# The first adaLN weights and the inputs, loaded in blocks of 256 columns

## The chip, the cores and the metric

The kernel runs on one core of one Trainium2 chip. The metric is the time of one execution on the device in microseconds (us). A core has the engines PE (TensorE: matrix products and transposes), ACT (ScalarE), DVE (VectorE), POOL (GpSimd) and SP (SyncE, which here only issues DMAs). They run side by side and wait for one another by semaphores. Sixteen DMA engines move data between the device memory and the on-chip memory, which has 128 partitions. PE writes to a separate accumulation memory of eight banks.

## The reference

One layer of a diffusion trunk on 128 context tokens and 512 latent tokens of width 1024, all in float32:

```
mod = silu(c) @ w_ada + b_ada             # 1024 x 6144; once for c, once for c_ctx
sh1, sc1, g1, sh2, sc2, g2 = split(mod)   # six pieces of 1024
h = x * (1 + sc1) + sh1
z = h @ w_in                              # 1024 x 3328, for three groups of heads
m = concat(attention A, gated recurrence B, attention C)(z) @ w_out
x = LN(alpha * x + g1 * m)
hid = relu((x * (1 + sc2) + sh2) @ w_ff1) ** 2
y = LN(alpha * x + g2 * (hid @ w_ff2))
```

Before anything of `w_in` can be multiplied, a block of 128 columns of the inputs needs its pieces of `sc1` and `sh1`, and these need their columns of `w_ada` over all 1024 rows.

## The kernel before, in words

The 640 tokens and the 1024 columns are cut into tiles of 128: `NT` = 5 tiles of tokens (tile 0 is the context) and `NK` = 8 blocks of columns. To reach float32 accuracy, each operand of a large product is split into a high and a low part (`split`: ACT copies the high part, DVE subtracts), and each product is three matmuls (`mm3`).

The change lies in the first stage, some 57 us long, a loop over the eight blocks j:

- `ada_load(j)` loads the columns of `sc1` and `sh1` of block j: two tiles of four row tiles each, two DMAs for each tile (256 KB, rows of 512 B), so 1 MB in four DMAs, all issued by SP. `x_load(j)` loads 128 columns of the inputs in two DMAs (64 and 256 KB). Three blocks are loaded ahead of the loop, and round j issues block j + 3. There are buffers for six blocks of weights and four of x.
- PE, block by block: `ada_rows` multiplies the conditioning with the 256 columns (sixteen instructions in the profile, `psada_s`); four transposes of the latent tiles of x (`psx`) and one of the context tile (`psm`); four small matmuls (L270, L271) that turn the adaLN rows into columns `sc1`, `sh1`.
- ACT scales and shifts the transposed block (`xm`, L275 and L276) and rounds it to `xh`; DVE subtracts for `xl`.
- `first_gemm(j - 2)` follows two blocks behind (`LAG` = 2): the products of block j - 2 with three columns of tiles of `w_in` (forget gates and q of group B, `wfq`), summed over all blocks in five banks `acc`. Their weights are loaded in rounds 0, 1, 3 and 5.

Behind the loop, PE multiplies the values of group B (`psib`, weights `wib`), and DVE and ACT work on the gates that come out of `acc`; `wfb` and `wq` are the next weights and `wad` the later columns of `w_ada`, in DMAs of 512 KB with 256 columns in a row (`ada_part`). All weights of `w_in` pass through `wslots`: two raw buffers, then the split into five buffers. SP issues in its own order, so a DMA that waits for a buffer holds those behind it. Six small constants (`scanm`, `rope_c`, `rope_s`, `gng`, `qng`, `kng`) are loaded by SP behind the stage.

What sets the order: in the loop the order on PE is written out by hand (`manual_schedule`). The other engines' order in the loop, and all engines' order behind it up to the output projection at some 420 us, is found by a planner when the kernel is built; it takes the program's order and estimated times, and lets an instruction that is ready pass one that waits. From the second half of the output projection on, all but POOL are in hand-written order again.

Of the kernel before, what the change touches and what calls it, by code (L numbers as in the profile page):

```python
# [11 lines left out]
F32 = mybir.dt.float32  # L12
# [7 lines left out]
P = 128  # L20
D = 1024
NK = D // P
NTOK = 640
NT = NTOK // P
# [38 lines left out]
def hybrid_layer_kernel(ctx: ExitStack, tc: tile.TileContext, T):  # L63
# [26 lines left out]
    def split(hi, lo, src):  # L90
        A.copy(hi, src)  # L91
        V.tensor_tensor(lo, src, f32(hi), op=ALU.subtract)  # L92
# [78 lines left out]
    with ExitStack() as sctx:  # L171
        sp = sctx.enter_context(tc.tile_pool(name="startsb", bufs=1, reuse_waits="tile"))

        crow = sp.tile([32, P], F32, tag="crow", name="crow")
        rows = sp.tile([37, P], F32, tag="rows", name="rows")
        nc.sync.dma_start(crow[0:8, :], T["c"])
        nc.scalar.dma_start(crow[8:16, :], T["c_ctx"])
        G.memset(cs.rearrange("p a b -> p (a b)"), 0.0)
        nc.scalar.dma_start(ident, T["k_ident"])
        nc.scalar.dma_start(crow[16:32, :], T["b_ada8"][0:16, :])  # L180
        ps0 = pp.tile([P, 512], F32, tag="misc", name="ps_rows", bufs=NMISC)
        PE.transpose(ps0[:, 0:32], crow, ident[0:32, 0:32])
        b1c = sp.tile([P, 16], F32, tag="b1c", name="b1c")
        V.tensor_copy(b1c, ps0[:, 16:32])
        sil = sp.tile([P, 16], F32, tag="sil", name="sil")
        sg = sp.tile([P, 16], F32, tag="sg", name="sg")
        A.activation(sg, ps0[:, 0:16], AF.Exp, scale=-1.0)
        V.tensor_scalar_add(sg, sg, 1.0)
        V.reciprocal(sg, sg)
        V.tensor_tensor(sil, ps0[:, 0:16], sg, op=ALU.mult)  # L190
        silv = sil.rearrange("p (v k) -> p k v", v=2)
        V.tensor_copy(cs[:, :, 0:2], silv)
        V.tensor_copy(cs[:, :, 16:18], silv)
        V.tensor_tensor(selc, ident[:, 0:2], ident[:, 32:34], op=ALU.add)
        V.tensor_tensor(selc, selc, ident[:, 64:66], op=ALU.add)
        V.tensor_tensor(selc, selc, ident[:, 96:98], op=ALU.add)

        def ada_load(j):
            parts = []
            for s in range(2):  # L200
                raw = sp.tile([P, 4, 2, P], F32, tag="adar0", name=f"adaw{j}_{s}", bufs=12)
                for i, c0 in enumerate((D + j * P, j * P)):
                    nc.sync.dma_start(
                        raw[:, :, i, :],
                        T["w_ada"][s * 512 : (s + 1) * 512, c0 : c0 + P].rearrange("(k p) n -> p k n", p=P),
                    )
                parts += [raw[:, k].rearrange("p a b -> p (a b)") for k in range(4)]
            return parts

        def x_load(j):  # L210
            x_j = sp.tile([P, NT, P], F32, tag="x", name=f"x{j}", bufs=4)
            csl = slice(j * P, (j + 1) * P)
            nc.sync.dma_start(x_j[:, 0, :], T["x_prompt"][:, csl])
            nc.sync.dma_start(x_j[:, 1:NT, :], T["x_sample"][:, csl].rearrange("(t p) n -> p t n", p=P))
            return x_j

        ahead = 3
        LAG = 2
        ada_q, x_q = [], []
        for j in range(ahead):  # L220
            ada_q.append(ada_load(j))
            x_q.append(x_load(j))
        acc = [pp.tile([P, 512], F32, tag=f"acc{i}", name=f"acc{i}") for i in range(5)]
        w01 = []

        def first_load(s):
            w01.extend(wslots(f"wfq{s}", T["w_in"], ((COL_FF, P), (COL_FB, P), (COL_QB, P)), 2, row0=s * 2 * P, nslot=1, swap=True))

        def first_gemm(j, cols):
            for i in cols:  # L230
                h, l = (w[:, i * P : (i + 1) * P] for w in w01[j])
                for st, mv, first, last in ((h, xh, True, False), (h, xl, False, False), (l, xh, False, True)):
                    PE.matmul(acc[i][:, 0:384], st, mv[:, j, 0:384], start=first and j == 0, stop=last and j == NK - 1)
                    PE.matmul(acc[3 + i // 2][:, i % 2 * 256 : i % 2 * 256 + 256], st, mv[:, j, 384:NTOK],
                              start=first and j == 0 and i != 1, stop=last and j == NK - 1 and i > 0,
                              skip_group_check=True)

        with tc.manual_schedule(engines={mybir.EngineType.PE}):
            for j in range(NK):
                ada, x_j = ada_q[j], x_q[j]  # L240
                if j in WPOS:
                    first_load(WPOS.index(j))
                if j + ahead < NK:
                    ada_q.append(ada_load(j + ahead))
                    x_q.append(x_load(j + ahead))
                if j == 2:
                    nc.gpsimd.dma_start(rows[0:8, :], T["ln1_g8"])
                    nc.gpsimd.dma_start(rows[8:16, :], T["ln1_b8"])
                    nc.gpsimd.dma_start(rows[16:17, :], T["subln_g"])
                    nc.gpsimd.dma_start(rows[17:21, 0:HD], T["lb_logits_fwd"])  # L250
                    nc.gpsimd.dma_start(rows[17:21, HD:P], T["lb_logits_bwd"])
                    nc.gpsimd.dma_start(rows[21:37, :], T["b_ada8"][24:40, :])
                    mf = sp.tile([P, 4 * CH], F32, tag="mf", name="mf")
                    nc.gpsimd.dma_start(mf, T["k_masks"])
                    G.tensor_copy(masks.rearrange("p a b -> p (a b)"), mf)
                if j == 6:
                    ps1 = pp.tile([P, 512], F32, tag="misc", name="ps_rows1", bufs=NMISC)
                    PE.transpose(ps1[:, 0:37], rows, ident[0:37, 0:37])
                    V.tensor_copy(colc, ps1[:, 0:37])
                    V.tensor_scalar_add(colc[:, 29:37], colc[:, 29:37], 1.0)  # L260
                r = sp.tile([P, 2 * P], F32, tag="adar", name=f"adar{j}", bufs=2)
                ada_rows(r, pp.tile([P, 512], F32, tag="ada", name=f"psada_s{j}", bufs=NADA), ada)
                px = pp.tile([P, 512], F32, tag="xt", name=f"psx{j}", bufs=NXT)
                for t in range(1, NT):
                    PE.transpose(px[:, (t - 1) * P : t * P], x_j[:, t, :], ident)
                pm = pp.tile([P, 512], F32, tag="misc", name=f"psm{j}", bufs=NMISC)
                PE.transpose(pm[:, 0:P], x_j[:, 0, :], ident)
                if j >= LAG:
                    first_gemm(j - LAG, (0,))
                PE.matmul(pm[:, P : P + 2], r[:, 0:P], selc, start=True, stop=True)  # L270
                PE.matmul(pm[:, P + 2 : P + 4], r[:, P : 2 * P], selc, start=True, stop=True)  # L271
                V.tensor_scalar(sc1[:, j, :], pm[:, P : P + 2], b1c[:, 8 + j : 9 + j], 1.0, op0=ALU.add, op1=ALU.add)
                V.tensor_scalar(sh1[:, j, :], pm[:, P + 2 : P + 4], b1c[:, j : j + 1], None, op0=ALU.add)
                xm = sp.tile([P, NTOK], F32, tag="xm", name=f"xm{j}", bufs=2)
                A.activation(xm[:, 0:P], pm[:, 0:P], AF.Identity, scale=sc1[:, j, 1:2], bias=sh1[:, j, 1:2])  # L275
                A.activation(xm[:, P:NTOK], px, AF.Identity, scale=sc1[:, j, 0:1], bias=sh1[:, j, 0:1])  # L276
                split(xh[:, j, :], xl[:, j, :], xm)
                if j >= LAG:
                    first_gemm(j - LAG, (1, 2))
            for j in range(NK - LAG, NK):  # L280
                first_gemm(j, range(3))
# [712 lines left out]
    gr, parts, tok, wks = {}, {}, {}, {}  # L994
# [102 lines left out]
    for h in range(NHA):  # L1097
        for t in range(1, NT):
            n = h * nu + t - 1
# [42 lines left out]
    for t in range(1, NT):  # L1142
        for j in range(4):
            n = NHA * nu + (t - 1) * 4 + j
# [60 lines left out]
    raws = {(i, j): rawp.tile([P, 4, HALF], F32, tag=f"q{i}{j}", name=f"q{i}{j}") for j in range(2) for i in range(2)}  # L1205
# [433 lines left out]
    for u in range(2, NU):  # L1639
# [32 lines left out]
        else:  # L1672
            c12(u - 1)

            f = f12[0].rearrange("p a k n -> p a (k n)")
# [71 lines left out]
    for n in range(2):  # L1747
# [6 lines left out]
        for m, i in enumerate(order):  # L1754
            if n == 0 and m < 4:
                continue
            if i % 2 == 0:
                w = next(ws)
                raw = ep.tile([P, 2, 512], F32, tag=f"wr{w % NWR}", name=f"wg{n}_{i}r")
# [111 lines left out]
```

## Time and profile before

| | |
|---|---|
| median of 3 runs | 940.05 us (936.37 to 941.13) |
| profiled execution | 940.01 us |
| its span, first to last instruction | 938.2 us |
| busy: PE, DVE, ACT, POOL | 880.3, 665.1, 474.9, 69.0 us |
| mean granted clock of PE | 0.975 of full speed |
| moved from and to device memory | 96.24 and 12.58 MB |

All times in the rows are microseconds from the start of the span unless marked ns. A busy PE is not PE at its peak, since matmuls overlap. The granted clock is 1.00 (2.4 GHz) or 0.50 (1.2 GHz); a mean between the two comes from a change inside the stretch. The DMA share is the mean busy share of the core's 16 DMA engines; it goes above 1 where packets overlap.

### The profile page before, as it was taken

To read this page: it belongs to the slowest core of one execution; us is meant where nothing else is said; L and a number is where in the kernel's file an instruction comes from. 1 tells how busy PE (TensorE), PEld (TensorE's weight loads), DVE (VectorE), ACT (ScalarE), POOL (GpSimd) and SP (SyncE) were. 2 spreads that over 40 slices of the span, in tenths; PEclk is the share of its full clock that TensorE was granted. 3 is DMA by queue.
4 is the path that set the end of the run, shared out by engine and by line. 5 is a ranking of instruction groups with operands and counts; after the bars stand their busy time and mean duration, and the time that the engine had idled before them with its cause. 6 is when DMAs were issued, how large, how long until landed. Compare 5 with 4: busy or idle time off the path is not lost.

```text
span 938.2 us, 15408 instructions
## 1 busy us (share of the span) xinstructions
PE 880.3 (94%) x5941; PEld 762.6 (81%) x5941; DVE 665.1 (71%) x1232; ACT 474.9 (51%) x973; POOL 69.0 (7%) x136
## 2 busy tenths in 40 slices
PE   5989898999999998999988899999998999999996
PEld 3878786789889786677778899988997888888885
DVE  2369997988876878886579877676762874574448
ACT  3567665466664638761566544453553633243320
POOL 2200010210101010001000100110000000000000
PEclk7999998999999999999999999999999999999998
DMA  9951525432122211007102543456325863052202
GB/s 261 287 168 50 179 71 146 118 95 69 55 58 62 68 51 57 2 28 274 36 1 64 186 145 134 157 176 208 129 79 188 295 218 99 22 177 90 67 22 92
DMA packets 102314, 109.84 MB, mean 117 GB/s; under 512 B 6720, under 2 KB 82208, under 8 KB 102240
## 3 DMA queue, kind: packets, MB, share of 16 engines
q1 hardware_dynamic: 96256, 92.33, 32.0%
q0 software_dynamic: 5792, 16.44, 5.0%
q8 instruction: 47, 0.77, 0.3%
q14 instruction: 27, 0.22, 0.1%
q10 hardware_dynamic: 192, 0.08, 0.0%
HBM read 96.24 MB, written 12.58 MB: 116 GB/s over the span
## 4 chain that ended last, share of the span: by engine, by line
PE 67%; DVE 15%; DMA 8%; ACT 6%; issue 3%; SPq 1%; DVEq 0%; ACTq 0%
PE psx L1453 10%; PE psy L131 8%; PE psy L129 8%; PE psy L130 8%; PE psz L1453 5%; DMA wad<-in_w_ada 3%; PE psA L130 2%; PE psA L129 2%; PE psA L131 2%; PE psavA L731 2%; DVE b_st L561 2%; PE psy L1453 2%; DMA wf_r<-in_w_ff 2%; PE psavC L953 1%; DVE b_lqk L516 1%
## 5 line engine op out<-in xcount | busy, mean ns | idle before, releaser
L92 DVE TENSOR_TENSOR gl<-hidb,gh 128x640 fp32r<-128x640 f32 x54 | 43.7, 821 | 49.1 <-ACT gh L91 49.0
L91 ACT CAST gh<-hidb 128x640 fp32r<-128x640 f32 x54 | 38.6, 728 | 69.3 <-PE psy L130 61.9
L1453 PE MATMUL psx<-s,wf3h 128*128 128x320 f32 x256 | 58.9, 317 | 6.2 <-ACT kept L1459 3.0
L129 PE MATMUL psA<-wa_h,xh 128*128 128x384 f32 x160 | 54.9, 344 | 0.0
L131 PE MATMUL psA<-wa_h,xl 128*128 128x384 f32 x160 | 54.5, 342 | 0.0
L130 PE MATMUL psA<-wa_l,xh 128*128 128x384 f32 x160 | 54.2, 340 | 0.0
L1459 ACT COPY kept<-psx 128x320 f32<-128x320 f32 x48 | 20.5, 427 | 65.6 <-PE psx L1453 65.6
L1453 PEld LDWEIGHTS psx<-s,wf3h 128*128 128x128 f32 x256 | 44.1, 193 | 7.0 <-ACT kept L1459 3.3
L1340 DVE TENSOR_TENSOR wf3l<-wf_t,wf3h 128x2048 fp32r<-128x2048 f32 (+2 forms) x20 | 37.2, 1864 | 9.0 <-ACT wf3h L1336 9.0
L1453 PE MATMUL psx<-s,wf3l 128*128 128x320 f32 x128 | 40.3, 315 | 0.0
L1472 DVE TENSOR_TENSOR st<-psz,kept 128x320 f32<-128x320 f32 x32 | 15.7, 489 | 26.2 <-ACT kept L1459 13.7
L129 PE MATMUL pswo<-wo,mxh 128*128 128x512 f32 x80 | 32.1, 403 | 0.4 <-ACT wo L91 0.4
L130 PE MATMUL pswo<-wo,mxh 128*128 128x512 f32 x80 | 31.7, 397 | 0.8 <-DVE wo L92 0.8
L709 DVE TENSOR_REDUCE nmA<-pssA 128x1 f32<-128x768 f32 x32 | 30.2, 951 | 2.2 <-PE pssA L707 1.8
L129 PEld LDWEIGHTS psA<-wa_h,xh 128*128 128x128 f32 x160 | 30.1, 188 | 1.9 <-issue 1.2
L1336 ACT CAST wf3h<-wf_t 128x2048 fp32r<-128x2048 f32 (+2 forms) x20 | 30.9, 1554 | 1.3 <-DVE wf_t L1312 0.9
L131 PE MATMUL pswo<-wo,mxl 128*128 128x512 f32 x80 | 31.5, 393 | 0.0
L1518 POOL DMA_DIRECT2D hd<-st x28 | 15.3, 546 | 219.3 <-ACT st L1465 120.4
L711 ACT ACTIVATE pA<-pssA,nmA 128x768 f32<-128x768 f32 x32 | 28.8, 903 | 3.3 <-DVE nmA L709 2.8
L130 PEld LDWEIGHTS psA<-wa_l,xh 128*128 128x128 f32 x160 | 30.2, 189 | 0.2
L131 PEld LDWEIGHTS psA<-wa_h,xl 128*128 128x128 f32 x160 | 30.1, 188 | 0.2
L1453 PE MATMUL psz<-s,wf3h 128*128 128x320 f32 x128 | 29.2, 315 | 0.0
(671 smaller groups left out, 2760.8 us busy)
## 6 DMA issues: line engine op xcount, KB each, us to landing
wad<-in_w_ada SPq DMA_DIRECT2D x32, 512.0 KB, 4.8
wf_r<-in_w_ff SPq DMA_DIRECT2D x32, 512.0 KB, 4.7
hd<-st POOLq DMA_DIRECT2D x28, 320.0 KB, 3.6
hidb<-hd SPq DMA_DIRECT2D x28, 320.0 KB, 4.7
adaw<-in_w_ada SPq DMA_DIRECT2D x32, 256.0 KB, 5.3
wa_r<-in_w_in SPq DMA_DIRECT2D x48, 128.0 KB, 2.7
wo_raw<-in_w_out SPq DMA_DIRECT2D x8, 512.0 KB, 6.5
x<-in_x_sample SPq DMA_DIRECT2D x8, 256.0 KB, 4.9
```

Of the source, the lines that this page charges most:

```text
L91: A.copy(hi, src)
L92: V.tensor_tensor(lo, src, f32(hi), op=ALU.subtract)
L129: PE.matmul(ps, s[0], m[0], start=start, stop=False)
L130: PE.matmul(ps, s[0], m[1], start=False, stop=False)
L131: PE.matmul(ps, s[1], m[0], start=False, stop=stop)
L561: V.scalar_tensor_tensor(dst, st[r, c, :], dec[r, c : c + 1], u(r, c), op0=ALU.mult, op1=ALU.add)
L709: V.tensor_reduce(nm, ps[:, 0:NKEY], axis=AX.X, op=ALU.max, negate=True)
L711: A.activation(pr, ps[:, 0:NKEY], AF.Exp, bias=nm, accum_out=sm[:, col : col + 1])
L1336: A.copy(h, src)
L1340: V.tensor_tensor(l, src, f32(h), op=ALU.subtract)
L1453: PE.matmul(ps, a_[:, k, :], b_[:, k, :], start=start and k == 0 and i == 0, stop=k == 3 and i == 2, skip_group_check=True)
L1459: A.copy(t, U[u].ps["x"][:, 0:HALF])
```

## The change

The weights and inputs of blocks 1 and 2, 3 and 4, 5 and 6 are loaded as pairs: each of the four weight DMAs of a pair brings 256 columns (512 KB, rows of 1 KB), and the two x DMAs bring 256 columns too. Blocks 0 and 7 stay alone. The order of the columns and the moment at which the loads are issued stay nearly the same: block 0 and the pair 1, 2 ahead of the loop, pair 3, 4 in round 0, pair 5, 6 in round 2, block 7 in round 4. Weight buffers: two tiles for single blocks and five for pairs (two tiles to a pair), as many bytes as before. Buffers of x: one single and two pairs. `ada_rows` gets its 256 columns as two runs of 128 in a wider tile.

```diff
-        def ada_load(j):
-            parts = []
+        SPANS = ((0, 1), (1, 2), (3, 2), (5, 2), (7, 1))
+
+        def ada_load(j0, nb):
+            raws = []
             for s in range(2):
-                raw = sp.tile([P, 4, 2, P], F32, tag="adar0", name=f"adaw{j}_{s}", bufs=12)
-                for i, c0 in enumerate((D + j * P, j * P)):
+                raw = sp.tile([P, 4, 2, nb * P], F32, tag=f"adar0{nb}", name=f"adaw{j0}_{s}", bufs=(0, 2, 5)[nb])
+                for i, c0 in enumerate((D + j0 * P, j0 * P)):
                     nc.sync.dma_start(
                         raw[:, :, i, :],
-                        T["w_ada"][s * 512 : (s + 1) * 512, c0 : c0 + P].rearrange("(k p) n -> p k n", p=P),
+                        T["w_ada"][s * 512 : (s + 1) * 512, c0 : c0 + nb * P].rearrange("(k p) n -> p k n", p=P),
                     )
-                parts += [raw[:, k].rearrange("p a b -> p (a b)") for k in range(4)]
-            return parts
+                raws.append(raw)
+            for b in range(nb):
+                ada_q[j0 + b] = [raws[k // 4][:, k % 4, :, b * P : (b + 1) * P] for k in range(NK)]
 
-        def x_load(j):
-            x_j = sp.tile([P, NT, P], F32, tag="x", name=f"x{j}", bufs=4)
-            csl = slice(j * P, (j + 1) * P)
+        def x_load(j0, nb):
+            x_j = sp.tile([P, NT, nb * P], F32, tag=f"x{nb}", name=f"x{j0}", bufs=(0, 1, 2)[nb])
+            csl = slice(j0 * P, (j0 + nb) * P)
             nc.sync.dma_start(x_j[:, 0, :], T["x_prompt"][:, csl])
             nc.sync.dma_start(x_j[:, 1:NT, :], T["x_sample"][:, csl].rearrange("(t p) n -> p t n", p=P))
-            return x_j
-
-        ahead = 3
+            for b in range(nb):
+                x_q[j0 + b] = x_j[:, :, b * P : (b + 1) * P]
+
         LAG = 2
-        ada_q, x_q = [], []
-        for j in range(ahead):
-            ada_q.append(ada_load(j))
-            x_q.append(x_load(j))
+        ada_q, x_q = {}, {}
+        for span in SPANS[0:2]:
+            ada_load(*span)
+            x_load(*span)
...
-                if j + ahead < NK:
-                    ada_q.append(ada_load(j + ahead))
-                    x_q.append(x_load(j + ahead))
+                for span in SPANS[2:]:
+                    if span[0] == j + 3:
+                        ada_load(*span)
+                        x_load(*span)
```

## Rows read from the trace of the kernel before

**Rows 1.** The page, engines' busy time, and shares of the chain.

```profile
PE 880.3 (94%) x5941; PEld 762.6 (81%) x5941; DVE 665.1 (71%) x1232; ACT 474.9 (51%) x973; POOL 69.0 (7%) x136
...
PE 67%; DVE 15%; DMA 8%; ACT 6%; issue 3%; SPq 1%; DVEq 0%; ACTq 0%
```

**Rows 2.** Stretches: length, busy PE PEld DVE ACT POOL, clock, DMA share, GB/s.

```profile
11.00:24.00 13.00, 10.25 (x60) 7.26 (x61) 3.64 (x11) 6.01 (x13) 0.00 (x0) 0.61 1.21 290
62.00:66.00 4.00, 3.13 (x27) 2.93 (x26) 2.36 (x5) 2.88 (x6) 0.00 (x0) 1.00 1.11 328
...
101.00:103.00 2.00, 2.00 (x44) 1.76 (x42) 1.94 (x7) 1.67 (x3) 0.00 (x0) 1.00 1.08 372
```

**Rows 3.** PE in order: start, length, line, op, out<-in, count [idle before <-releaser].

```profile
11.38 0.64 PE L144 MATMUL psada_s<-adaw,cs 128*32 128x256 f32 x8 [0.57 <-DMA adaw<-in_w_ada]
13.19 0.64 PE L144 MATMUL psada_s<-adaw,cs 128*32 128x256 f32 x8 [1.17 <-DMA adaw<-in_w_ada]
14.32 1.08 PE L265 MATMUL psx<-ident,x 128*128 128x128 f32 x4 [0.49 <-ACT adar L146]
...
16.19 1.08 PE L144 MATMUL psada_s<-adaw,cs 128*32 128x256 f32 x8
17.95 1.08 PE L144 MATMUL psada_s<-adaw,cs 128*32 128x256 f32 x8 [0.68 <-DMA adaw<-in_w_ada]
19.06 1.09 PE L265 MATMUL psx<-ident,x 128*128 128x128 f32 x4
```

**Rows 4.** PE in order, later in the stage and behind it.

```profile
26.31 1.58 PE L144 MATMUL psada_s<-adaw,cs 128*32 128x256 f32 x16
...
36.40 1.07 PE L144 MATMUL psada_s<-adaw,cs 128*32 128x256 f32 x16
...
42.79 0.63 PE L265 MATMUL psx<-ident,x 128*128 128x128 f32 x4 [0.35 <-DMA x<-in_x_sample]
...
47.77 0.63 PE L265 MATMUL psx<-ident,x 128*128 128x128 f32 x4 [0.16 <-PE psada_s L144]
...
57.06 0.28 PE L129 MATMUL psib<-wib_h,xh 128*128 128x256 f32 x1
```

**Rows 5.** Stretches again, for the clock and the planned part.

```profile
13.00:14.00 1.00, 0.64 (x8) 0.19 (x8) 0.79 (x1) 0.30 (x2) 0.00 (x0) 0.88 1.22 291
14.00:27.00 13.00, 11.97 (x60) 9.27 (x64) 3.48 (x10) 5.35 (x11) 0.00 (x0) 0.50 1.21 290
27.00:28.00 1.00, 1.00 (x14) 0.37 (x7) 0.00 (x0) 0.03 (x1) 0.00 (x1) 0.80 1.22 291
...
72.00:75.00 3.00, 3.00 (x20) 2.66 (x19) 2.90 (x12) 2.59 (x9) 0.00 (x0) 0.50 0.00 0
...
76.00:360.00 284.00, 271.73 (x2371) 235.75 (x2368) 240.09 (x575) 170.20 (x438) 30.07 (x52) 0.99 0.30 89
```

**Rows 6.** SP's queue in order of time: DMA issues.

```profile
4.85 3.47 SPq L203 DMA_DIRECT2D adaw<-in_w_ada  x4
...
26.89 3.54 SPq L203 DMA_DIRECT2D adaw<-in_w_ada  x4
...
53.84 0.37 SPq L109 DMA_DIRECT2D wfb_r<-in_w_in  x1
...
57.73 1.54 SPq L109 DMA_DIRECT2D wfb_r<-in_w_in  x3
...
98.85 2.68 SPq L968 DMA_DIRECT2D wad<-in_w_ada  x4
```

**Rows 7.** Groups of instructions in the first 75 us: busy, mean ns.

```profile
L144 PE MATMUL psada_s<-adaw,cs 128*32 128x256 f32 x128 | 11.5, 466 | 4.1 <-DMA adaw<-in_w_ada 2.4 <-DVE cs L193 1.6
...
L265 PE MATMUL psx<-ident,x 128*128 128x128 f32 x32 | 6.5, 338 | 1.0 <-ACT adar L146 0.5 <-DMA x<-in_x_sample 0.3 <-PE psada_s L144 0.2
```

**Rows 8.** ACT in order of time.

```profile
50.49 0.46 ACT L275 ACTIVATE xm<-psm,sh,sc 128x128 f32<-128x128 f32 x1 [0.87 <-DVE sh L273]
...
63.12 0.40 ACT L91 CAST wfb_h<-wfb_r 128x256 fp32r<-128x256 f32 x1 [1.75 <-DMA wfb_r<-in_w_in]
```

## The prediction, made before the changed kernel was run

> **What bounds the kernel now.** I read the page's first part and its chain first: PE is busy for 880.3 of 938.2 us and carries 67% of the chain [rows 1], so time lost on PE early on is not made up later unless an idle stretch takes it in. Then the windows of the stage that the change touches, the first 57 us. From 11 to 24 us the DMA engines move 290 GB/s at a share of 1.21, the most that they do anywhere in that stage, while PE is busy 10.25 of 13 us [rows 2]: the stage is fed by the DMA at its start. PE in order of time shows where that ends [rows 3]: block 1 waits for its weights at 11.38 (0.57 us) and 13.19 (1.17), block 2 at 17.95 (0.68). From 19.06 (the first transpose of block 2) PE runs on without a gap to speak of, but for two waits: 0.35 us for the inputs of block 6 and 0.16 us in block 7 [rows 4]. So from about 19 us PE bounds the stage, and the loads only just keep up.
>
> The granted clock is at half (1.2 of 2.4 GHz) from about 13.9 to 27.4 us, after PE had stood still more than it worked, and full again once PE had worked without a gap [rows 5]. The first products of block 0 and the adaLN of blocks 2 and 3 run at that half.
>
> **The change part by part.** The bytes, the order of the blocks on PE and the number of instructions on PE, ACT and DVE stay. What moves is when a block is there.
>
> *Rate.* Blocks 1 to 6 are read in rows of 1 KB. Nothing in the first stage shows their rate, but the later adaLN loads `wad` read the same tensor in the same form (512 KB, 256 columns): with four of them issued [rows 6] the rate is 372 GB/s [rows 2]. A stretch in which rows of 512 B and of 1 KB mix gave 328 [rows 2]. The ends for the new loads are 290 (nothing gained; a loss has no reason, as the rows only become longer) and 372. I take 372 for the weights and, as no load of x in wide rows exists in the trace, 328 for x.
>
> The Trainium skill, on the page "DMA: Bandwidth & Descriptors" (section "Why small descriptors are slow (HBM only)"), gives a fixed overhead of about 3 cycles for a packet beside one for each 32 bytes. An estimate from that page: 19 cycles for 512 B and 35 for 1 KB, 9% more per second, 316 GB/s; block 1's inputs would then land at 18.3 and the sum below would be +2.8 us. The two windows above differ by 28%, so the trace does not agree that the overhead is so small, and I go by it.
>
> *Block 1 arrives later.* It now needs the whole pair: 2.10 MB of weights and 0.66 MB of x, where its own 1.05 MB and 0.33 MB did. The second half of its weights was there at 13.19 [rows 3], 1.05 MB behind the end of block 0; at 290 GB/s that is 3.62 us, so block 0's loads end at 9.57. From there: 2.10/0.372 = 5.64 us and 0.66/0.328 = 2.00 us, so the inputs of blocks 1 and 2 land at 17.2. At 290 throughout it is 9.49 us, at 19.06, which is where block 2's were before; at 372 it is 16.97.
>
> *What is late next.* PE's order is written by hand, so all of block 1 behind its weights waits for x: four transposes, one more, and four small matmuls, which took from 14.32 to 16.19, 1.87 us. Behind them stand block 2's sixteen adaLN matmuls, two times 1.08 us at half clock [rows 3]. Before, they were done in the gaps of the loads; now they start at 17.2 and end at 17.2 + 1.87 + 2.2 = 21.3, where block 2's transposes began at 19.06: **+2.2 us** (at 372 throughout +2.0, at 290 +4.1). All of PE's work behind is pushed by this. I take the half clock as ending after the same work as before, so the whole 2.2 stay; if it ended at the same moment, half of them would come back (+1.1).
>
> *Later blocks.* After 17.2 come wfq0 (0.39 MB at 290: 1.36 us), the pair 3 and 4 (7.64), wfq1 (1.36) and the pair 5 and 6 (7.64), which end at 26.2 and 35.2. PE came to block 3 at 26.31 and to block 5 at 36.40 [rows 4], and comes 2.2 later now. Even at 290 the ends are 30.0 and 40.8 for the x of the two pairs; PE, then 4.1 late, asks for it a block's adaLN (1.5 and 1.0 us) behind 30.4 and 40.5. So no later pair waits, and the waits of blocks 6 and 7 go: **-0.5 us** [rows 4].
>
> *Buffers and SP.* DMA issues fall from 48 to 30. SP spends 3.47 us on four of them [rows 6] while the transfers are saturated, so the issues are hidden: 0. Pair 5 takes the buffers of pair 1: its second half of weights waits for the first eight adaLN matmuls of block 2, its x for block 2's transposes, over by about 23. SP came to this place at 26.89 [rows 6]. Cover is 4 us. Were it gone, wfq2, block 7, wfq3 and wib would stand behind the waiting DMA, and PE would wait at block 5.
>
> *Moving operand in two runs.* The adaLN matmul now reads its 256 columns as two runs of 128. No row shows that. Between 0 and two matmuls of 128 in place of one of 256 (twice 338 against 466 ns, 45% of the 8.6 us that six of the eight blocks take [rows 7]: +3.9), I take 0, by the row of the 256 columns themselves, which stay as many.
>
> *Behind the stage.* ACT's and DVE's orders are set by a planner, not by the diff. With those of before, ACT's `xm` of block 7 (50.49) comes behind PE, then `wib_h` and DVE's `wib_l`, then the buffer for `wfb_r`, whose first part SP issues at 53.84 and its second behind six constants at 57.73; it lands at 63.12, and ACT has stood for 1.75 us until then [rows 6, 8]. This chain hangs on PE's block 7, so it moves along with it.
>
> **Sum:** +2.2 - 0.5 = +1.7 us. The profiled execution took 940.01 us (span 938.2 and 1.8 around it), the same as the median of 940.05, so 941.7. That is 0.2%, under the 0.5% that a measurement of this kernel can tell from no change. This case's own range, from the ends of the rate and of the clock: 940.5 to 943.7.
>
> **The rivals.**
> *The early data also removes ACT's stall.* wfq3 and wib land some 4 us sooner at the higher rate. If the planner then puts the casts of wib ahead of `xm` of block 7, `wfb_r` is issued before PE gets there, and the 1.75 us on ACT [rows 8] go. +1.7 - 1.75: 940.0. For it: ACT does nothing else in them. Against: the chain that follows also hangs on PE's last products of the stage, which are late.
>
> *Wide rows are no faster, and the clock rises later: slower.* If 290 GB/s is what reading this tensor at the saturated start allows, block 1's x lands at 19.06 and PE is 4.1 us late. PE then stands from 11 to 19 with little work, and if the full clock comes one step later (the next stretch at half, around 72 to 75 [rows 5], is at least 3 us long), half of it or more, 1.7 us, is lost: 4.1 - 0.5 + 1.7 = +5.3, 945.3. It decides from x of block 1 landing at 19 on with the clock still at half at 30. For it: the saturated share of 1.21 with rows of 512 B shows that something else than the packets may limit. Against: 372 GB/s from the same tensor.
>
> *The planner orders the stretch behind anew.* From 57 to some 420 us the order is planned, from the program and estimated times, and these change with the loads. From 76 to 360 us PE stands idle for 284.0 - 271.7 = 12.3 us [rows 5]. An order that saves half of that gives 940.0 + 1.7 - 6.1 = 935.6; one that adds as much 947.8. For it: SP issues a part of `wfb_r` ahead of six constants that stand before it in the program, and the rest behind them [rows 6]. Against: the start is one block in front of everything, and a plain delay reorders nothing.
>
> **How the numbers follow.** Forecast 0.45 (941.7). ACT's stall gone 0.15 (940.0). Slow rows and late clock 0.15 (945.3, of which 0.12 beyond 0.5%, which is 944.75). New order 0.25: 0.13 faster than 935.35, 0.07 slower, 0.05 between. Faster 0.13; within 0.5% 0.45 + 0.15 + 0.03 + 0.05 = 0.68; slower 0.12 + 0.07 = 0.19. The range 935.5 to 946.5 leaves out most of the 0.13 below and some 0.06 above.
>
> **What would show it.** Right: more than 330 GB/s between 10 and 17 us; block 1's transposes near 17 and block 2's near 21; no wait for x in blocks 6 and 7; the first matmul of `psib` at 58 to 60 and `wfb_h` on ACT at 64 to 65. Wrong: 290 GB/s there; block 2's transposes at 19 or before; a DMA wait in blocks 3 to 6; or the same shift at 57 us and another total, which puts the cause in the planned stretch.

## The result, and the profile after

The changed kernel takes 947.91 us (median of 15 runs, 944.9 to 951.82); the kernel before, run beside it, 941.31 (15 runs, 936.37 to 945.25). The ratio is 1.0073 [1.0054, 1.0092]: slower by 0.7%, and outside the range of the prediction (941.7, up to 946.5). The profiled execution of after took 951.45 us, 3.5 above its median; that of before 940.01, 1.3 below. A difference of the two traces (11.4 us) is therefore larger than that of the medians (6.6).

The page of after, busy time and shares of the chain, beside [rows 1]:

```profile
PE 885.0 (93%) x5941; PEld 768.9 (81%) x5941; DVE 664.9 (70%) x1232; ACT 474.2 (50%) x973; POOL 69.1 (7%) x136
...
PE 70%; DVE 13%; DMA 8%; ACT 6%; issue 2%; SPq 1%; DVEq 0%; ACTq 0%
```

The same instructions, and PE busy for 4.7 us more. The next view says where the rest is: stretches of after, with the columns of [rows 2]. The first answers to 11 to 24 us there, the second to 76 to 360 us in [rows 5] (11 us longer, as its end comes 11 us later).

```profile
11.00:24.00 13.00, 8.43 (x52) 5.47 (x53) 3.26 (x9) 5.37 (x11) 0.00 (x0) 1.00 1.10 343
...
76.00:371.00 295.00, 277.31 (x2328) 241.44 (x2326) 238.15 (x569) 167.04 (x431) 30.13 (x52) 0.96 0.28 84
```

At the start 343 GB/s instead of 290. In the planned stretch PE is busy 277.31 instead of 271.73 us, at a mean clock of 0.96 instead of 0.99, and stands still for 295.00 - 277.31 = 17.7 us instead of 12.3. So about 5.4 us of the 11 are new waits, and 5.6 are work that takes longer at the half clock. The split is rough: at 76 us PE of after is some 40 matmuls further than before, so the two stretches do not hold quite the same work.

PE in order of time, after, beside [rows 3, 4]:

```profile
12.93 1.08 PE L144 MATMUL psada_s<-adaw,cs 128*32 128x256 f32 x8 [2.05 <-DMA adaw<-in_w_ada]
15.82 1.08 PE L144 MATMUL psada_s<-adaw,cs 128*32 128x256 f32 x8 [1.81 <-DMA adaw<-in_w_ada]
...
17.73 1.09 PE L270 MATMUL psx<-ident,x 128*128 128x128 f32 x4 [0.83 <-DMA x<-in_x_sample]
...
19.61 1.93 PE L144 MATMUL psada_s<-adaw,cs 128*32 128x256 f32 x16
21.47 1.11 PE L270 MATMUL psx<-ident,x 128*128 128x128 f32 x4
...
24.91 0.67 PE L237 MATMUL acc<-xh,wfq_h 128*128 128x384 f32 x1
25.37 0.34 PE L238 MATMUL acc<-xh,wfq_h 128*128 128x256 f32 x1
...
27.11 1.07 PE L144 MATMUL psada_s<-adaw,cs 128*32 128x256 f32 x16
...
47.45 0.66 PE L270 MATMUL psx<-ident,x 128*128 128x128 f32 x4
...
56.42 0.28 PE L129 MATMUL psib<-wib_h,xh 128*128 128x256 f32 x1
```

Block 1's transposes start at 17.73, block 2's at 21.47 (19.06 before: 2.4 late), block 3's adaLN at 27.11 (26.31 before: 0.8 late), and block 7's transposes at 47.45 (47.77 before: 0.3 early, with no wait). The first `psib` comes at 56.42, 0.6 us before its old time. The stage that was changed loses nothing. In the ten traces with the new loads (after and nine of the experiments below) the first `psib` comes between 55.3 and 56.8 us, in the three with the old ones between 57.1 and 58.3.

Behind it the engines run in another order. Compared instruction by instruction, 149 of PE's 5105 (as the program counts them; the profile has 5941), 102 of DVE's 1232, 78 of ACT's 896 and 8 of SP's loads stand elsewhere, all between some 50 and 240 us but for a few of DVE's and ACT's in the stage itself. One of the first shows in SP's queue of after, beside [rows 6]: two parts of `wfb_r` are issued at 50.98 (one at 53.84 before).

```profile
22.50 4.78 SPq L206 DMA_DIRECT2D adaw<-in_w_ada  x4
...
50.98 0.92 SPq L109 DMA_DIRECT2D wfb_r<-in_w_in  x2
...
55.84 1.01 SPq L109 DMA_DIRECT2D wfb_r<-in_w_in  x2
```

(The row at 22.50 is the weights of blocks 5 and 6.) ACT of after, beside [rows 8], takes the first cast of `wib_h` ahead of `xm` of block 7, and the casts of four parts of `wfb_h` together at 56.53:

```profile
47.95 1.06 ACT L91 CAST wib_h<-wib_r 128x1024 fp32r<-128x1024 f32 x1
49.92 0.46 ACT L280 ACTIVATE xm<-psm,sh,sc 128x128 f32<-128x128 f32 x1 [0.91 <-DVE sh L278]
...
56.53 1.33 ACT L91 CAST wfb_h<-wfb_r 128x256 fp32r<-128x256 f32 x4 [3.41 <-DMA wfb_r<-in_w_in]
...
62.63 0.40 ACT L91 CAST wfb_h<-wfb_r 128x256 fp32r<-128x256 f32 x1
```

To find where the time goes, the start of each DVE instruction was compared with the start of the same one in the trace of before. After is 1.1 us late at 164 us (time of before), 9.3 at 172, 11.0 at 206, and stays near there to the end (11.2). One place makes most of it: the state of head 2 of group B (`psu2` on PE, then `b_st` on DVE) beside tile 2 of head 0 of group A (`psA02`, 24 products on PE, then `zA02` on DVE). PE of before, with the columns of [rows 3]:

```profile
166.97 0.64 PE L144 MATMUL psada<-wad,cs 128*32 128x256 f32 x8 [0.19 <-DMA wad<-in_w_ada]
167.54 0.66 PE L554 MATMUL psu<-mixed,b_kht 64*128 64x64 f32 x8
...
168.67 0.89 PE L554 MATMUL psu<-mixed,b_kht 64*128 64x64 f32 x12
169.49 0.44 PE L129 MATMUL psA<-wa_h,xh 128*128 128x384 f32 x1
...
173.78 0.38 PE L489 MATMUL pskht<-ident,b_kq 128*128 128x128 f32 x2
```

DVE of before:

```profile
170.06 4.34 DVE L561 SCALAR_TENSOR_TENSOR b_st<-b_st,b_dec,psu 64x64 f32<-64x64 f32 x14 [0.25 <-ACT b_st L564]
```

All of `psu2` is made by 169.5; then PE works 4.3 us on `psA02` while DVE works 4.34 us on the state. PE of after:

```profile
169.87 0.64 PE L144 MATMUL psada<-wad,cs 128*32 128x256 f32 x8 [1.75 <-DMA wad<-in_w_ada]
170.44 0.66 PE L559 MATMUL psu<-mixed,b_kht 64*128 64x64 f32 x8
...
171.57 0.66 PE L559 MATMUL psu<-mixed,b_kht 64*128 64x64 f32 x8
172.16 0.62 PE L129 MATMUL psA<-wa_h,xh 128*128 128x384 f32 x1
172.58 0.52 PE L130 MATMUL psA<-wa_l,xh 128*128 128x384 f32 x1
...
178.09 0.43 PE L559 MATMUL psu<-mixed,b_kht 64*128 64x64 f32 x2
```

ACT of after, whose copy starts the state:

```profile
178.56 0.21 ACT L568 COPY b_st<-psu 64x64 f32<-64x64 f32 x1 [4.77 <-PE psu L559]
```

DVE of after:

```profile
178.20 0.42 DVE L623 TENSOR_TENSOR zA<-psA,rope_c 128x256 f32<-128x256 f32 x1 [5.00 <-PE psA L131]
...
179.02 0.28 DVE L566 SCALAR_TENSOR_TENSOR b_st<-b_st,b_dec,psu 64x64 f32<-64x64 f32 x1
...
179.66 4.04 DVE L566 SCALAR_TENSOR_TENSOR b_st<-b_st,b_dec,psu 64x64 f32<-64x64 f32 x13
```

The last product of `psu2` now stands behind `psA02`, and on DVE `zA02` stands ahead of the state. DVE waits 5.00 us for what PE does, and the state starts at 179.02 instead of 170.06. The 9.0 us can nearly be added up on PE: it comes to `psu2` 2.9 us later (170.44 for 167.54, of which 1.6 is a longer wait for `wad`), `psA02` ahead of the last product costs 4.3, and the half clock in it (the products take 0.52 instead of 0.33) 1.6 more. The sum is 8.8.

### The profile page after: what moved, and what is told of

It is laid out like the page before. It is cut to its first block, busy times and chain, and to the rows that moved or that the text cites. A ratio compares the mean times of both kernels' runs of the same rounds, so it can differ in the third digit from the quotient of the medians.

```text
span 949.6 us, 15369 instructions
## 1 busy us (share of the span) xinstructions
PE 885.0 (93%) x5941; PEld 768.9 (81%) x5941; DVE 664.9 (70%) x1232; ACT 474.2 (50%) x973; POOL 69.1 (7%) x136
## 4 chain that ended last, share of the span: by engine, by line
PE 70%; DVE 13%; DMA 8%; ACT 6%; issue 2%; SPq 1%; DVEq 0%; ACTq 0%
PE psx L1458 9%; PE psy L131 8%; PE psy L130 8%; PE psy L129 8%; PE psz L1458 5%; DMA wad<-in_w_ada 3%; PE psA L129 2%; PE psA L130 2%; PE psA L131 2%; PE psavA L736 2%; DMA wf_r<-in_w_ff 2%; PE psy L1458 2%; PE psavC L958 1%; DVE b_st L566 1%; DVE b_lqk L521 1%
```

## The experiments

Each was timed beside the kernel before (6 to 12 runs each, after 15; before takes 941.31 us beside after, 940.5 beside experiments 1 to 8 and 941.7 beside 9 to 11). "DVE late" is the start of the same DVE instruction less that in the trace of before, at three times of that trace, from the one profiled execution of each.

| kernel | median, us | ratio to before [95%] | 164 us | 189 us | 243 us |
|---|---|---|---|---|---|
| after | 947.91 | 1.0073 [1.0054, 1.0092] | +1.1 | +9.3 | +11.0 |
| 1 new loads, old order | 938.48 | 0.9983 [0.9960, 1.0007] | +0.5 | +0.2 | +0.2 |
| 2 old loads, new order | 950.31 | 1.0096 [1.0066, 1.0126] | +3.2 | +9.0 | +10.7 |
| 3 new order, state first | 949.69 | 1.0099 [1.0065, 1.0133] | +1.6 | +8.0 | +10.7 |
| 4 old order, state split | 946.84 | 1.0068 [1.0043, 1.0094] | -0.4 | +5.5 | +5.5 |
| 5 new window only | 947.44 | 1.0080 [1.0051, 1.0109] | -0.7 | +8.3 | +8.3 |
| 6 old window only | 946.03 | 1.0057 [1.0031, 1.0082] | -1.4 | +0.9 | +2.7 |
| 7 new first part only | 942.39 | 1.0021 [0.9996, 1.0045] | +1.5 | +4.0 | +4.0 |
| 8 new last part only | 942.51 | 1.0016 [0.9994, 1.0037] | +1.1 | +1.9 | +3.6 |
| 9 window, PE only | 949.36 | 1.0079 [1.0051, 1.0108] | -2.4 | +8.3 | +8.3 |
| 10 window, DVE only | 946.32 | 1.0051 [1.0029, 1.0073] | +1.0 | +6.7 | +6.8 |
| 11 window, ACT and SP only | 940.53 | 0.9991 [0.9970, 1.0012] | +0.4 | +2.7 | +2.7 |

**1 and 2: the loads or the order?** A list of each engine's instructions is held against the planner: every instruction depends on the one ahead of it in the list, with no semaphore added. Experiment 1 is the changed kernel with the order of before on PE, DVE, ACT and SP; experiment 2 is the kernel before with the order of after.

```diff
+def hold_order(tc):
+    for eng, spec in HELD.items():
...
+                cur = seen[-r]
+                if prev is not None:
+                    tc.add_manual_dep(cur, prev.name, mybir.DependencyInfo(mybir.DependencyClass.NoSync, mybir.DependencyReason.DATA), reason="held order")
+                prev = cur
...
         hybrid_layer_kernel(tc, aps)
+        hold_order(tc)
```

> The loads of the change, with every instruction behind them held in the order of the kernel before on PE, DVE, ACT and SP. If the order of the planned stretch cost the time, this runs as the kernel before within 0.3%: 938 to 943 us. If the loads themselves cost it (block 1 late, as forecast), it stays at 946 to 949 us.

> The loads of the kernel before, with every instruction behind them held in the order of the changed kernel. If the order cost the time: 946 to 950 us. If the loads cost it: 939 to 943 us.

The order carries all of it: the new loads in the old order are level with before (0.9983, with 1 in the interval), and the old loads in the new order lose as much as the change does. The new loads in the old order also leave the planned stretch as it was, in PE's busy time and its clock [rows 5]; the stretch from 76 to 360 us of experiment 1:

```profile
76.00:360.00 284.00, 271.21 (x2361) 235.29 (x2358) 239.55 (x575) 169.87 (x437) 30.08 (x52) 0.99 0.30 89
```

**3 and 4: is it that one place?** Experiment 3 repairs it in the order of after; experiment 4 breaks it in the kernel before by the reverse of this edit. The lists hold numbers; here and below they are shown in short, by tiles.

```diff
 PE   psu2 (9 of 10)
+PE   psu2 (the 10th)
 PE   psA02 (24)
-PE   psu2 (the 10th)
-DVE  zA02 (2), b_st (1), zA02 (1), b_st (13), b_stn (2)
+DVE  b_st (14), b_stn (1), zA02 (2), b_stn (1), zA02 (1)
```

> The changed kernel in its own order, but for four places: the last state product of head 2 (psu) goes ahead of the 24 products of psA in front of it, and DVE's three rope steps of that psA tile go behind the state chain. If this one place costs the 8 us by which DVE's rows jump near 170 us: 939 to 942 us. If the loss is spread over the whole new order: 945 to 948 us. If it is the loads: 946 to 949 us.

> The kernel before in its own order, but for the same four places: the last state product of head 2 goes behind the 24 products of psA, and DVE's rope steps of that tile ahead of the state chain. If this one place costs the time: 945 to 949 us. If it does not: 940 to 943 us.

Broken in the kernel before, the place costs 5.5 us on DVE and 0.7% in the time: DVE waits 4.16 us for `psA02`, and PE then 4.05 for the state. DVE of experiment 4:

```profile
173.48 0.42 DVE L618 TENSOR_TENSOR zA<-psA,rope_c 128x256 f32<-128x256 f32 x1 [4.16 <-PE psA L131]
```

PE of experiment 4:

```profile
179.75 0.72 PE L500 MATMUL psl<-b_kq,b_k 64*64 64x64 f32 x16 [4.05 <-DVE b_stn L561]
```

Repaired in the order of after, it gives nothing back (949.69, above all three ranges). Of the 9.3 us, 3.4 are left at 172 us, but two places behind take up what was saved. DVE waits for `psl` of head 3, which the new order puts behind products of `psA03` (8.0 us late at 189), and then PE waits for ACT's `cqkA` (10.7 at 243). So the idea that this place costs all fell; it costs, but is not alone. DVE of experiment 3:

```profile
173.47 4.34 DVE L566 SCALAR_TENSOR_TENSOR b_st<-b_st,b_dec,psu 64x64 f32<-64x64 f32 x14 [0.94 <-ACT b_st L569]
...
183.65 0.30 DVE L545 COPY_PREDICATED b_att<-masks,psl 128x128 f32<-128x128 uint8 x1 [3.24 <-PE psl L505]
```

PE of experiment 3:

```profile
203.72 0.80 PE L784 MATMUL pscs<-cqkA 64*128 64x128 f32 x4 [3.20 <-ACT cqkA L704]
```

**5 to 8: which stretch of the order?** At two positions on each engine, `c1` (about 169 us) and `c2` (about 186 us), both orders have the same instructions behind them, so they can be cut and joined there. All four have the new loads; the lists are the old order but for

```diff
-HELD = before[:c1] + before[c1:c2] + before[c2:]
+HELD = before[:c1] + after[c1:c2] + before[c2:]
```

in experiment 5, `after, before, after` in 6, `after, before, before` in 7 and `before, before, after` in 8.

> New loads; the order on PE, DVE, ACT and SP is that of before up to about 169 us, that of after in the window that runs from there to about 186 us (state of head 2, tiles psA02 and psA03), and that of before again behind it. Theory A, the loss is made in this window: 947 to 949 us, and DVE starts the state of head 2 some 9 us later than in the run with the old order throughout, and stays 8 to 10 us late to the end. Rival B, it takes the whole new order (the stretch from 57 us on brings the engines into the window differently, or the stretch behind it): 940 to 943 us. Rival C, the window costs what the one product and the three rope steps cost in the old order by themselves: 944 to 946.

> The counterpart: new loads, the order of after up to about 169 us, that of before in the window to about 186 us, that of after behind it. Theory A: the loss goes but for the 2 us that the stretch behind adds (DVE +9 to +11 between 190 and 206 us): 939 to 942 us. Rival B (a place behind takes up what is saved, as when the product alone was put back): 947 to 950 us, with DVE no more than 3 us late at 190 us and 8 to 10 us late at 210.

> New loads, the order of after from 57 to about 169 us and that of before from there on. Theory A: nothing is lost there: 938 to 940.5 us (DVE within 1 us of before at 168 us). Rival (the reordering of the first part, with its later weights wad, brings the loss about): 945 us or more.

> New loads, the order of before up to about 186 us and that of after from there on (which changes up to some 230 us). Theory A: only the 2 us that DVE lost between 200 and 206 us: 939.5 to 942 us. Rival B, the place at 202 to 206 us (PE's pscs behind ACT's cqkA) loses as much by itself once the window ahead of it loses nothing: 945 to 949 us.

The window of 17 us is enough: alone it gives 1.0080, as much as the whole, and DVE 8.3 us late. That is theory A of experiment 5. Experiment 6 met neither theory. Its trace is what A said (0.9 us late at 189, 2.7 at 243), but its median, 946.0, lies between the two: with the window put back, the ratio only falls from 1.0073 to 1.0057. DVE loses 3.3 us more between 409 us and the end, where the order is the same. The rows say what that is: the same stretch of before, of experiment 6 and of experiment 1, each from the same DVE instruction on:

```profile
409.00:938.20 529.20, 501.70 (x2762) 441.74 (x2760) 347.62 (x474) 228.29 (x362) 25.38 (x47) 0.98 0.38 128
411.20:943.80 532.60, 505.49 (x2762) 444.88 (x2760) 347.92 (x474) 228.34 (x362) 25.46 (x47) 0.97 0.37 127
409.20:935.90 526.70, 498.83 (x2762) 439.68 (x2760) 347.35 (x474) 228.19 (x362) 25.37 (x47) 0.99 0.37 129
```

PE stands still for 27.5, 27.1 and 27.9 us; what differs is how long the same 2762 matmuls take, 501.70, 505.49 and 498.83 us, and the granted clock goes with it. So in that trace it is no wait behind the window but more time at the half clock. Why experiment 6 gets it is open; over its nine runs the mean clock is 0.976 (median), and 0.981 for before beside it.

The other two parts were taken too lightly. DVE comes out of the first 4.0 us late, after this wait of PE for `wad` (1.06 before) and a clock of 0.61 from 165 to 170 us. PE of experiment 7:

```profile
162.89 1.08 PE L144 MATMUL psadag<-wad,cs 128*32 128x256 f32 x8 [2.77 <-DMA wad<-in_w_ada]
```

DVE comes out of the last part 3.6 us late, 2.7 more than at 172 us, ahead of it (0.9). In the changed kernel this is where the delay goes from 9.3 to 11.0: ACT takes a cast of `wa_h` behind `pscA` (3.65 us of wait) and comes late to `cqkA`, for which PE waits 3.09 us (0.87 before). PE of after:

```profile
205.06 0.49 PE L784 MATMUL pscs<-cqkA 64*128 64x128 f32 x4 [3.09 <-ACT cqkA L704]
```

ACT of after:

```profile
202.22 0.83 ACT L91 CAST wa_h<-wa_r 128x768 fp32r<-128x768 f32 x1 [3.65 <-PE pscA L702]
```

For these two the medians alone (1.0021 and 1.0016, both with 1 in the interval) can't tell a loss from none. The parts don't add up either: 8.3 + 4.0 + 3.6 = 15.9 us late against 11.0 for all three. A delay that is there already may hide a later one; this was not tried.

**9 to 11: which engine in the window?** New loads, the old order, and in the window the order of after on PE (9), on DVE (10), or on ACT and SP (11). The lists are shortened to what moves; each experiment takes its own lines.

```diff
-PE   psu2 (10), psA02 (24), pskht3, pslv3, psadag2304 (1), psl3 (8), psadag2304 (7), psA03 (4), pslv3, psA03 (20)
+PE   psu2 (9), psA02 (24), psu2 (1), pskht3, pslv3, psadag2304 (8), psA03 (17), psl3 (8), psA03 (7), pslv3
-DVE  b2, b_st (14), b_stn (1), zA02 (2), b_stn (1), zA02 (1)
+DVE  b2, a2, b2, zA02 (2), b_st (1), zA02 (1), b_st (13), b_stn (2)
-ACT  ada5, b_d (1), zA01, b_d (1), b_st (2), b_d (2)
+ACT  b_d (2), ada5, zA01, b_d (2), b_st (2)
-SP   wad2560, wa1 (3), wad2560, wa1 (3), wad4352 (2)
+SP   wad2560, wa1 (1), wad2560, wa1 (3), wad4352 (2), wa1 (2)
```

> New loads and the order of before everywhere, but for PE in the window from about 169 to 186 us, which has that of after there (the last product of the state of head 2 behind the 24 of psA02, the 24 of psA03 ahead of psl of head 3). Theory A, PE's order makes the loss: DVE starts the state of head 2 some 5 to 9 us later than with the old order, and the time is 944 to 948 us. Rival, it takes DVE's order too (the rope steps of zA02 ahead of the state): no more than 3 us, 939 to 942.

> The same, but DVE alone has the order of after in the window: a2 and the steps on zA02, which need PE's psA02, stand ahead of the state of head 2, while PE still makes the state's products ahead of psA02. Theory A: DVE waits for psA02, 24 products of 0.33 us and so at most some 5 us behind the state's products; the state itself is late by that: 940 to 944 us. Rival, DVE's order alone makes the loss: 945 or more.

> The same, but ACT and SP alone have the order of after in the window (SP issues one pair of wad two loads earlier, ACT two copies of masks earlier). Theory A: nothing, 937.5 to 940.5 us, DVE within 1 us of the run with the old order. Rival, the weights wad that PE waited for at 169.87 us in the changed kernel (1.75 us) come late by SP's order: 941 or more.

PE's order alone costs as much as the window (8.3 us late, 1.0079; 949.36 is above the 948 of theory A); DVE's alone costs 6.8 us and 0.5%, which is the rival of experiment 10 and not its theory A; ACT's and SP's nothing that can be measured (0.9991), though the trace shows 2.7 us in the window. The rows tell why PE's and DVE's don't add. With PE's order (17 of the 24 products of `psA03`, not all, stand ahead of `psl`), DVE waits 4.85 us until the last product behind `psA02` is there, and PE then 4.58 us for the buffer of `psA03`, which `zA02` frees behind the state; later DVE waits 5.16 us for `psl`. DVE of experiment 9:

```profile
172.01 4.33 DVE L566 SCALAR_TENSOR_TENSOR b_st<-b_st,b_dec,psu 64x64 f32<-64x64 f32 x14 [4.85 <-ACT b_st L569]
...
184.46 0.31 DVE L545 COPY_PREDICATED b_att<-masks,psl 128x128 f32<-128x128 uint8 x1 [5.16 <-PE psl L505]
```

PE of experiment 9:

```profile
171.09 0.43 PE L559 MATMUL psu<-mixed,b_kht 64*128 64x64 f32 x2
...
178.44 0.69 PE L129 MATMUL psA<-wa_h,xh 128*128 128x384 f32 x1 [4.58 <-ACT zA L759]
```

With DVE's order it is DVE that waits for `psA02`, with the state's products long made, and PE that waits for the state. DVE of experiment 10:

```profile
175.33 0.43 DVE L623 TENSOR_TENSOR zA<-psA,rope_c 128x256 f32<-128x256 f32 x1 [4.00 <-PE psA L131]
```

PE of experiment 10:

```profile
181.44 0.48 PE L505 MATMUL psl<-b_kq,b_k 64*64 64x64 f32 x16 [4.40 <-DVE b_stn L566]
```

Either way the two pieces of some 4.3 us that ran side by side run one behind the other. The stretch from 164 to 184 us of before, with the columns of [rows 2]:

```profile
164.00:184.00 20.00, 19.32 (x224) 15.93 (x226) 18.58 (x61) 8.55 (x27) 3.56 (x7) 1.00 0.43 133
```

The same stretch of experiment 9:

```profile
164.00:184.00 20.00, 14.96 (x137) 12.88 (x133) 9.86 (x35) 3.36 (x11) 1.13 (x2) 0.83 0.34 108
```

PE and DVE, both busy for over 18 of the 20 us before, drop to 15.0 and 9.9. The PE time that is left also runs in part at the half clock, behind the wait of 4.58 us (0.83 in the mean; the next products of `psA03` take 0.52 us).

The version that joins what was good in both kernels is experiment 1: clearly ahead of the changed kernel, and not measurably ahead of the one before.

## Why the prediction was wrong, point by point

**The rate: right.** More than 330 GB/s between 10 and 17 us was the sign, and 344 is there (343 from 11 to 24, for 290 before [rows 2]); the inputs of block 1 were to land at 17.2, and its transposes started at 17.73. The Trainium skill's page "DMA: Bandwidth & Descriptors" (section "Why small descriptors are slow (HBM only)") names a fixed overhead of about 3 cycles for a packet, from which 9% for the longer rows and 316 GB/s were estimated; measured are 343/290 = 18%. The trace does not agree that the overhead is so small, as the row for `wad` had said.

**Block 1 late, and block 2 behind it: right, then gone.** Block 2's transposes were to start at 21.3 and started at 21.47. But "I take the half clock as ending after the same work as before, so the whole 2.2 stay" failed: the products become short at 25.37, where the stretch at half lasted to about 27.4 before [rows 5]. The loads do this: in the ten traces with the new loads the granted clock rises to full between 21.9 and 25.5 us, in the three with the old ones between 27.3 and 27.5. Block 3 was 0.8 us late instead of 2.2. With the waits of blocks 6 and 7 gone, as forecast, nothing was left by block 7. Experiment 1 is this part of the change by itself: its interval ends at 1.0007, and the sum of +1.7 us was 1.0018. So the stage was forecast too slow, by more than its measurement is uncertain.

**Buffers, SP, the moving operand: right in what they cost, with less cover than was said.** SP came to the weights of blocks 5 and 6 at 22.50, not at 26.89, 1 us behind the end of block 2's adaLN matmuls (21.5), so the 4 us of cover were not there; but PE did not wait. Sixteen adaLN matmuls of two runs of 128 columns take 1.07 us at 27.11, as with one run of 256 at 36.40 [rows 4], and blocks 3 to 6 wait for no DMA.

**ACT's stall, the first rival: its condition came, its time did not.** `wib_h` is cast at 47.95, ahead of `xm` of block 7 at 49.92 (50.49 before, with `wib_h` behind it), and `wfb_r` is issued 2.9 us sooner. But ACT still waits for `wfb_r` (3.41 us at 56.53, for four parts together), and the kernel takes 947.9, not 940.0: this was one of many moves of the planner.

**Behind the stage: this is the step that failed.** The sum took the planned stretch as unchanged, so that it only moves along with PE's block 7, and put it at nothing. "With those of before", the orders of ACT and DVE, was the condition, and it did not hold. The first `psib` was not late but 0.6 us early, and the first `wfb_h` came at 56.53, in a group of four, where one at 64 to 65 was to be seen. That the planner might order the stretch anew was the third rival, with 0.07 for the slower side. Its price of +6.1 us came from half of PE's idle time there; the 947.8 that it gave is near the measured median, but not by its working, since about half of the loss is longer work at the half clock; that the two numbers are near is luck. Its mechanism is what the runs show: the +1.7 us that the forecast took from the start are not there, and all of the loss is in the order: the old loads in the new order lose 1.0% (experiment 2), the new loads in the old order nothing (experiment 1, 0.9983). The 17 us around the state of head 2 are enough to make it (5), and there PE's order alone (9). What is not shown is that the loss goes when only these 17 us are put back (6).

**What misled.** "A plain delay reorders nothing" was argued from how the start looks, not from a row. The planner doesn't take a delay: it takes another program, with other loads and buffers in front, and 8 of SP's loads and 149 of PE's instructions came out elsewhere. Which of its estimates tipped was not tried, and stays open. The prediction had also named the sign, the same time at 57 us and another total, so the trace could be read against it at once.

## What to carry to other kernels

Where a planner orders the instructions, an edit that is free where it stands can still cost 0.7% a hundred microseconds behind: give a new order a real chance, of either sign, and compare the two orders before the two times. To tell an edit from its reordering, hold the old order with the edit, and the new order without it. And a good order in such a stretch lives on pairs of engines working side by side: look for one product that releases a long chain on the other engine, and see that nothing long stands ahead of it.

## What the runs showed of the hardware that was not expected

- The granted clock in the trace can miss a stretch. In after it is given as 1.00 from 11 to 24 us, while eight adaLN matmuls take 1.08 us at 12.93 and 15.82, the length that they have in the stretch at 0.50 before [rows 3, 5], and short products only begin at 25.37. So it is in before: the clock is given as 0.99 from 5 to 13.9 us, while sixteen adaLN matmuls take 2.26 us at 6.96 and 1.07 at 36.40 [rows 4]. The lengths of like matmuls are the better witness.
- Stretches with the same order on every engine differ by some microseconds between single executions. From 409 us to the end DVE gains 2.7 us on before in experiment 1 and loses 3.3 in experiment 6, and nearly all of it is the time of PE's same matmuls at a granted clock of 0.99 and 0.97, for 0.98 before. The delay at one instruction tells more than the total of one trace.
